# Twenty latency numbers of an order planner, in a hybrid retention and gated-delta layer

## The chip, the cores and the metric

The kernel runs on one core of a Trainium2 chip. The metric is the device time of one execution in microseconds (us), as a median over runs. The core has a matrix engine (TensorE, PE in the profile; its weight loads are PEld), a vector engine (VectorE, DVE), a scalar engine (ScalarE, ACT), a general engine (GpSimd, POOL) and a queue engine (SyncE, SP) that here issues DMAs alone. Each engine works through its own instructions in program order; semaphores hold an instruction until what it needs is there.

## The reference

One decoder layer over 2048 new tokens and, beside them, 8 sample sequences of 8 tokens with states of their own. Half of the heads are retention heads, half gated delta-rule heads; one input projection feeds both, one output projection joins them, and a squared-ReLU MLP follows. Norms stand before and after each half of the layer.

```
h = rmsnorm(x);  q_r, k_r, v_r, gate_r, qkv_g, z_g, a_g, b_g = split(h @ w_in)
retention (4 heads, 128 x 128 state):   q, k rotated by position;  S_t = gamma S_{t-1} + k_t^T v_t;  o_t = q_t S_t
gated delta (4 heads, 128 x 128 state): conv of width 4 and silu on q, k, v;  q, k l2-normed
    g = -exp(A_log) softplus(a + dt_bias);  beta = sigmoid(b)
    S_t = exp(g_t) (I - beta_t k_t k_t^T) S_{t-1} + beta_t k_t v_t^T;  o_t = q_t^T S_t
x = x + rmsnorm([rmsnorm(o_r) silu(gate_r), rmsnorm(o_g) silu(z_g)] @ w_out)
x = x + rmsnorm(square(relu(rmsnorm(x) @ w_up)) @ w_down)
```

Both head groups are computed in chunks. For a chunk of the delta rule the inverse of a triangular matrix I + A is wanted.

## The kernel before

**Tiling.** The 2048 tokens go through in four blocks of 512 (block 0 to 3), each as four chunks or tiles of 128. Block 1 also carries the 64 sample rows, as a fifth tile. A float32 product is made from a rounded part and a remainder (`fhi`, `flo`; `bhi`, `blo`; `ahi`, `alo`; weights as `wpc`), so that three products stand for one; the remainders are made on DVE. All matmuls are issued at L271, all transposes at L275, and most DVE work by helpers at L256 and L259, so tiles rather than lines tell rows apart.

**Two kinds of PE work.** The main stream is the dense work: input projection of a block (`proj`, four kinds of units for four heads), the MLP of the block before it (`mlp`: 8 groups, each an up half and a down half, `mlp_down`, of two units), `out_proj`, and the last MLP group. `merge` interleaves the projection units of block b with the MLP units of block b-1, by which of them may start. Block 0 has no MLP before it, block 3's MLP runs alone at the end. Main products go to three PSUM buffers (`mm`). Beside it run the side steps, small chains that go back and forth between PE and DVE, ACT or POOL: `gdn_head`, `ret_head`, `gdn_sample`, `ret_sample`, `norm2`, `gate_scalars` and others. Their PSUM buffers are the five `mx`, which ACT also uses as scratch when it squares something for a norm.

**What sets the order.** The program is written by a planner, the class `Weave`, that has a clock of its own, `W.t`. The clock runs forward by a fixed cost at each PE product (L271 and L275), and only by these. A side step that has issued its PE products and the other engines' work behind them yields a number, its estimate of the time until its next PE products have their data. When the planner's clock has passed that estimate, the side's next PE products are written into PE's order, between two main products. PE's order is kept as it is written; a product put too early holds the whole of PE back until its data is there, and one put late delays its own chain. DVE's, ACT's and POOL's orders are set by a scheduler, which sees the same program. The estimates stand in the table `TUNE` (L103 to L121), in us of the planner's clock: `first` for block 0, `samp` for block 1, `rest` for blocks 2 and 3.

**The names that the change touches**, each the estimate for the next PE products:

- `inv`: the first transposes of the inverse of a delta-rule head (L834). In blocks 1 to 3, `small_blocks` (L892) makes the inverses of the 16 x 16 diagonal blocks ahead of them, on DVE and by DMAs that POOL issues; its last operations are the products `ym<-ym,cst` and `XX<-XX,ym` on DVE.
- `g5`: the transposes of each further level of that inverse wait a step ahead of the products at L843. In block 0 there are six levels.
- `c1`, `c2`, `c3`: the three steps of the recurrence over chunks, at L866, L871 and L859 (tiles `R`, `vn`, `Sg`).
- `r0`: the first transposes of a retention head (L1148), of the rotated keys (`mt` in blocks 1 to 3, parts of `a`, `flo` and other pages in block 0). DVE rotates them.
- `s3`, `s4`: two steps of the inverse of the sample rows in block 1 (tiles `mss` and `Ys`).
- `h2`: the transposes of a tile after the norm ahead of the MLP (`norm2`, L1349); the tile's pages are `ym`, `XX`, `mt`, `kv` or `a`.

Other gates bear on the prediction. `gate_scalars` makes the decays of all heads of a block (`gp`, `g`) on DVE, after the first `g` unit of `proj`; `ret_sample` needs the rotated sample rows (`qks`). In `out_proj` (L1270) the first three tiles are multiplied with six of the eight heads; the products with the last two heads wait for their outputs, which come through DRAM as `bhi` and `blo`.

The two lines of the planner that decide, in `_step`:

```
w = next(e[1])
e[0] = self.t + w if isinstance(w, float) else w
```

Of the kernel before, what the change touches and what calls it, by code (L numbers as in the profile page):

```python
# [92 lines left out]
def rope_table(nb):  # L93
# [8 lines left out]

TUNE = dict(  # L103
    first=dict(
        conv=7.29, inv=5.0, mem=7.63, pace=0.08, gate=10.83, h2=10.56, rstd=16.8, hk=1.57, put=1.7, gate2=1.82, sc=2.02, gs=9.72,
        g1=2.55, g2=2.75, g3=0.91, g4=2.06, g5=0.58, c1=1.61, c2=1.07, c3=0.99, glate=4.36, s1=7.06, s2=1.58, s3=0.83,
        s4=1.43, s5=0.98, s6=0.86, s7=1.7, r0=2.61, rs=1.89, r1=1.4, r2=2.98, r3=0.73, rlate=6.88, t1=7.35, t2=0.71,
        st=3.5, dg=1.65, n0=0.08, n1=2.49, n2=3.62, n3=1.1, f0=0.1, f1=1.8, f2=1.2),
    samp=dict(
        conv=16.33, inv=44.0, mem=5.28, pace=2.29, gate=12.82, h2=16.26, rstd=0.08, hk=3.65, put=2.29, gate2=1.7, sc=0.68, gs=23.38,  # L110
        g1=2.52, g2=2.04, g3=1.15, g4=1.79, g5=2.54, c1=0.79, c2=1.26, c3=1.4, glate=4.36, s1=4.54, s2=1.63, s3=1.09,
        s4=1.96, s5=1.36, s6=1.13, s7=2.24, r0=1.05, rs=2.27, r1=1.05, r2=1.7, r3=1.68, rlate=4.44, t1=6.0, t2=1.67,
        st=4.16, dg=0.41, n0=0.1, n1=3.78, n2=1.5, n3=1.35, f0=0.1, f1=2.43, f2=1.0),
    rest=dict(
        conv=26.24, inv=40.0, mem=5.1, pace=1.94, gate=16.02, h2=10.82, rstd=20.79, hk=3.86, put=1.19, gate2=1.8, sc=0.53, gs=17.96,
        g1=1.52, g2=1.9, g3=1.26, g4=1.3, g5=1.47, c1=1.22, c2=1.02, c3=0.75, glate=5.39, s1=8.4, s2=3.68, s3=1.36,
        s4=0.84, s5=0.59, s6=1.99, s7=1.22, r0=1.35, rs=1.96, r1=1.15, r2=1.06, r3=1.01, rlate=6.52, t1=9.72, t2=1.51,
        st=6.48, dg=3.52, n0=0.09, n1=2.8, n2=0.84, n3=1.08, f0=0.1, f1=1.15, f2=1.0),
    seq0='g0 r0 v0 q0 q1 v1 q2 g1 v2 r1 q3 v3 g2 r2 g3 r3',
    seq1='q0 q1 g0 r0 v0 g1 r1 v1 g2 q2 r2 v2 q3 g3 r3 v3',  # L120
# [1443 lines left out]
```

## Time and profile before

| | us |
|---|---|
| median of 3 runs | 3024.33 |
| lowest and highest run | 3021.01, 3025.94 |
| the profiled execution | 3030.91 |
| its span in the trace | 3029.1 |
| PE busy | 2879.0 (95%) |
| DVE, ACT, POOL busy | 1443.0, 966.2, 826.9 |
| granted clock of PE, mean | 0.98 |

A span is the time from the first to the last instruction in the trace. In the chain of work that ended last PE holds 77% of the span, DVE 11%, DMA 5%. "Idle" of PE is time between the modelled end of one product and the start of the next; the trace names the engine, tile and line whose result ended it. The granted clock of PE is at one of two levels, 1.0 (2.4 GHz) or 0.50 (1.2 GHz); a stretch that holds both has a value between. Block 0 runs from 0 to about 415 us, with its output projection to 475; block 1 with block 0's MLP to 1172, its output projection to 1285; blocks 2 and 3 to 2660; block 3's MLP to the end.

### The profile page before, as it was taken

The page shows a single profiled execution, that of the slowest core. Times are in us where ns is not written, and L with a number is a line of the kernel's source. Part 1 is how long each engine was busy: PE and PEld are TensorE (multiplying, and loading weights), DVE is VectorE, ACT ScalarE, POOL GpSimd, SP SyncE. Part 2 cuts the span into 40 slices and gives each one's busy share as a digit, 9 for nine tenths or more (in the row PEclk, how much of TensorE's full clock was granted, in tenths as well). Part 3 has the DMA queues.
Part 4 walks back from the last instruction along what each step waited for, and adds up shares of the span by engine and source line. Part 5 has one row for each costly group of instructions (what it writes and reads, how often), then busy time and mean ns, then how long its engine had stood idle before and what let it go on. Part 6 is the DMA issues. An engine that isn't in the chain of part 4 may idle for free.

```text
span 3029.1 us, 43658 instructions
## 1 busy us (share of the span) xinstructions
PE 2879.0 (95%) x16392; PEld 2490.3 (82%) x16392; DVE 1443.0 (48%) x3074; ACT 966.2 (32%) x2573; POOL 826.9 (27%) x970
## 2 busy tenths in 40 slices
PE   7989889899989989899999999999999999999998
PEld 6778788686978779688988989978888888888887
DVE  6655466647483642655254544265353635332113
ACT  4555433233232432332222332332222222221111
POOL 6444232536162541602020211131121212120000
PEclk9999899999999999899999999999999999999999
DMA  8445374656555665764444454675555555665554
GB/s 318 174 160 178 129 273 150 200 187 231 173 196 200 211 222 202 274 224 152 161 161 168 152 193 154 211 257 172 173 193 181 180 180 190 225 246 182 186 195 170
DMA packets 190771, 589.48 MB, mean 195 GB/s; under 512 B 26816, under 2 KB 33344, under 8 KB 190560
## 3 DMA queue, kind: packets, MB, share of 16 engines
q1 hardware_dynamic: 157520, 498.36, 47.6%
q0 software_dynamic: 31888, 86.24, 8.6%
q8 instruction: 129, 2.11, 0.3%
q10 hardware_dynamic: 1152, 2.10, 0.2%
q14 instruction: 82, 0.67, 0.1%
HBM read 443.35 MB, written 138.05 MB: 192 GB/s over the span
## 4 chain that ended last, share of the span: by engine, by line
PE 77%; DVE 11%; DMA 5%; issue 3%; POOL 2%; ACT 2%; SPq 0%; DVEq 0%; POOLq 0%; ACTq 0%
PE mm L271 66%; PE mx L271 8%; PE mx L275 2%; DVE XX L259 1%; DVE ym L259 1%; POOL wpc L259 1%; DVE raw L259 1%; DVE mt L259 1%; DMA x1d<-mt 1%; DMA xin<-in_w_out 1%; DMA wpc<-ws 0%; DVE a L259 0%; DVE flo L259 0%; DMA xin<-in_w_down 0%; DVE blo L256 0%
## 5 line engine op out<-in xcount | busy, mean ns | idle before, releaser
L271 PE MATMUL mm<-ahi,wpc 128*128 128x512 f32 (+2 forms) x3040 | 874.9, 362 | 1.9 <-POOL wpc L259 1.9
L271 PE MATMUL mm<-wpc,fhi 128*128 128x512 f32 x2048 | 659.6, 403 | 17.2 <-POOL wpc L259 7.0
L271 PEld LDWEIGHTS mm<-ahi,wpc 128*128 128x128 f32 x3040 | 542.7, 190 | 81.5 <-issue 6.6
L271 PE MATMUL mm<-alo,wpc 128*128 128x512 f32 (+2 forms) x1520 | 538.1, 354 | 2.0 <-DVE alo L259 2.0
L271 PEld LDWEIGHTS mm<-wpc,fhi 128*128 128x128 f32 x2048 | 382.7, 191 | 106.6 <-POOL wpc L259 9.2
L271 PE MATMUL mm<-bhi,wpc 128*128 128x512 f32 (+2 forms) x1536 | 427.8, 354 | 3.7 <-DMA wpc<-ws 3.7
L271 PE MATMUL mm<-wpc,flo 128*128 128x512 f32 x1024 | 408.6, 399 | 10.3 <-DVE flo L259 10.3
L259 POOL TENSOR_TENSOR wpc<-xin,wpc 128x512 fp32r<-128x512 f32 (+1 forms) x208 | 277.3, 1348 | 190.7 <-ACT wpc L253 180.0
L253 ACT ACTIVATE raw<-mm 128x512 f32<-128x512 f32 (+2 forms) x226 | 114.9, 509 | 633.5 <-PE mm L271 617.4
L271 PEld LDWEIGHTS mm<-alo,wpc 128*128 128x128 f32 x1520 | 288.8, 190 | 34.2 <-DVE alo L259 2.2
L271 PEld LDWEIGHTS mm<-bhi,wpc 128*128 128x128 f32 x1536 | 276.0, 191 | 36.1 <-DMA wpc<-ws 3.9
L271 PE MATMUL mm<-wpc,bhi 128*128 128x256 f32 (+1 forms) x1664 | 295.2, 283 | 1.1 <-ACT bhi L253 1.1
L259 DVE TENSOR_TENSOR a<-a,mm 128x512 f32<-128x512 f32 x224 | 152.5, 685 | 256.1 <-PE mm L271 255.5
L271 PE MATMUL mm<-blo,wpc 128*128 128x512 f32 (+2 forms) x768 | 266.4, 347 | 0.0
L259 DVE TENSOR_TENSOR flo<-raw,fhi 128x512 fp32r<-128x512 f32 (+1 forms) x166 | 108.9, 656 | 330.4 <-ACT raw L253 329.8
L271 PEld LDWEIGHTS mm<-wpc,bhi 128*128 128x128 f32 x1664 | 250.3, 188 | 2.2 <-ACT bhi L253 1.4
L271 PEld LDWEIGHTS mm<-wpc,flo 128*128 128x128 f32 x1024 | 195.2, 191 | 57.3 <-DVE flo L259 12.3
L271 PE MATMUL mm<-wpc,blo 128*128 128x256 f32 (+1 forms) x768 | 214.7, 280 | 0.2 <-DVE blo L259 0.2
L253 ACT ACTIVATE wpc<-xin 128x512 fp32r<-128x512 f32 (+1 forms) x208 | 129.8, 629 | 203.2 <-PE mm L271 119.6
L271 PEld LDWEIGHTS mm<-blo,wpc 128*128 128x128 f32 x768 | 147.4, 192 | 14.7
L271 PEld LDWEIGHTS mm<-wpc,blo 128*128 128x128 f32 x768 | 144.5, 188 | 0.4 <-DVE blo L259 0.4
L253 ACT ACTIVATE XX<-mx 128x512 f32<-128x512 f32 x62 | 36.9, 595 | 305.0 <-PE mx L275 304.9
(504 smaller groups left out, 3965.2 us busy)
## 6 DMA issues: line engine op xcount, KB each, us to landing
wpc<-ws SPq DMA_DIRECT2D x612, 512.0 KB, 5.0
ws<-wpc SPq DMA_DIRECT2D x204, 512.0 KB, 5.7
xin<-in_w_up SPq DMA_DIRECT2D x64, 256.0 KB, 5.4
xin<-in_w_down SPq DMA_DIRECT2D x64, 256.0 KB, 5.4
xin<-in_x_prompt POOLq DMA_DIRECT2D x56, 256.0 KB, 5.0
xin<-in_w_ret SPq DMA_DIRECT2D x28, 256.0 KB, 4.3
mixd<-raw POOLq DMA_DIRECT2D x25, 256.0 KB, 4.4
xin<-mixd POOLq DMA_DIRECT2D x25, 256.0 KB, 4.0
```

Source lines behind the costliest of these rows:

```text
L253: return A.activation(out, in_, f, **kw)
L259: return (eng or V).tensor_tensor(out=out, in0=a, in1=b, op=op)
L271: return tc.keep_in_program_order(nc.tensor.matmul(out, lhsT, rhs, start=start, stop=stop))
L275: return tc.keep_in_program_order(nc.tensor.transpose(out, in_, ident[:rows, :rows]))
```

## The change

Twenty numbers of the table `TUNE` are raised; nothing else is edited. The program has the same products, the same operations on the other engines and the same DMAs. What differs is the place of PE products in PE's order, and by it the order in which the scheduler puts the other engines' work.

```diff
     first=dict(
-        conv=7.29, inv=5.0, ... h2=10.56, ...
-        ... g5=0.58, c1=1.61, c2=1.07, c3=0.99, ...
-        ... r0=2.61, ...
+        conv=7.29, inv=9.5, ... h2=15.0, ...
+        ... g5=1.0, c1=2.0, c2=1.4, c3=1.6, ...
+        ... r0=4.5, ...
     samp=dict(
-        conv=16.33, inv=44.0, ...
-        ... s3=1.09,
-        s4=1.96, ... r0=1.05, ...
+        conv=16.33, inv=50.0, ...
+        ... s3=3.5,
+        s4=4.5, ... r0=4.0, ...
     rest=dict(
-        ... h2=10.82, ...
-        ... r0=1.35, ...
+        ... h2=13.5, ...
+        ... r0=2.6, ...
```

(The first number of a list and its neighbours are shown where they help to find the place; unchanged entries are left out.)

How the order moves is seen in three places. On PE, at the end of block 1's MLP in block 2, `norm2` puts the transposes of its first tile (the page `XX`). Before, they stand right behind a tile of `mlp_down` and ahead of the products of the sample rows (`fs`):

```order
L271 MATMUL mm_18814<-wpc_18743,fhi_17880 128x512 x2
L271 MATMUL mm_18814<-wpc_18743,flo_17881 128x512
L275 MATMUL mx_18844<-cst,XX_18273 128x128 x4
L275 MATMUL mx_18851<-cst,XX_18273 128x128 x4
L271 MATMUL mm_18860<-wpc_18737,fs_17882 128x512 x2
L271 MATMUL mm_18860<-wpc_18739,fs_17882 128x512 x2
L271 MATMUL mm_18860<-wpc_18741,fs_17882 128x512 x2
L271 MATMUL mm_18860<-wpc_18743,fs_17882 128x512 x2
```

and now:

```order
L271 MATMUL mm_18811<-wpc_18740,fhi_17877 128x512 x2
L271 MATMUL mm_18811<-wpc_18740,flo_17878 128x512
L271 MATMUL mm_18841<-wpc_18734,fs_17879 128x512 x2
L271 MATMUL mm_18841<-wpc_18736,fs_17879 128x512 x2
L271 MATMUL mm_18841<-wpc_18738,fs_17879 128x512 x2
L271 MATMUL mm_18841<-wpc_18740,fs_17879 128x512 x2
L271 MATMUL mm_18862<-wpc_18854,fhi_17877 128x512 x2
L271 MATMUL mm_18862<-wpc_18854,flo_17878 128x512
L271 MATMUL mm_18862<-wpc_18856,fhi_17877 128x512 x2
L271 MATMUL mm_18862<-wpc_18856,flo_17878 128x512
L275 MATMUL mx_18871<-cst,XX_18270 128x128 x4
L275 MATMUL mx_18878<-cst,XX_18270 128x128 x4
```

The transposes now have the eight `fs` products and six of the next unit ahead of them.

On PE, in block 1 at its first retention head, the transposes of the rotated keys (`mt`), the first products of the gate (`g`, 128x16) and the transpose of the rotated sample rows (`qks`) stand close together. Before:

```order
L271 MATMUL mm_4837<-bhi_3561,wpc_4831 128x256
L275 MATMUL mx_4850<-cst,mt_4652 128x128 x4
L271 MATMUL mx_4856<-g_4690,cst 128x16
L271 MATMUL mx_4856<-g_4690,Lr 128x16
L271 MATMUL mx_4856<-g_4690,ones 128x16
L275 MATMUL mx_4872<-cst,qks_4653 64x128
```

and now, with ten projection products left out between the two pieces:

```order
L271 MATMUL mx_4853<-g_4690,cst 128x16
L271 MATMUL mx_4853<-g_4690,Lr 128x16
L271 MATMUL mx_4853<-g_4690,ones 128x16
L271 MATMUL mm_4837<-bhi_3561,wpc_4833 128x256
L271 MATMUL mm_4837<-blo_3562,wpc_4833 128x256
L271 MATMUL mm_4837<-bhi_3561,wpc_4833 128x256
L275 MATMUL mx_4872<-cst,qks_4653 64x128
```

```order
L271 MATMUL mm_4882<-bhi_3561,wpc_4829 128x320
L271 MATMUL mx_4889<-g_4690,cst 64x4
L271 MATMUL mx_4889<-g_4690,Lsr 64x4
L271 MATMUL mx_4889<-gb_4859,ones 128x32
L271 MATMUL mx_4897<-Ss_4864,Lsr 64x256 x2
L275 MATMUL mx_4903<-cst,mt_4652 128x128 x4
```

The transposes of `mt` have moved behind the gate's and the sample rows' first steps, which now come first.

On DVE, in block 1 at the end of `small_blocks` of the last head, the last reductions, the accumulations of the MLP's down products (`a<-a,mm`) and the two last operations ahead of the inverse stand so before:

```order
L259 TENSOR_TENSOR a_1108_5499<-a_1108_5499,mm_10489 128x512
L928 TENSOR_REDUCE ym_10049<-ym_10049 128x32
L259 TENSOR_TENSOR ym_10049<-ym_10049 128x512
L996 COPY Ys_10355<-mx_10517 64x64
L928 TENSOR_REDUCE ym_10049<-ym_10049 128x32
L259 TENSOR_TENSOR a_1109_5500<-a_1109_5500,mm_10509 128x512
L259 TENSOR_TENSOR ym_10049<-ym_10049,cst 128x512
L259 TENSOR_TENSOR XX_10007<-XX_10007,ym_10049 128x512
```

and now:

```order
L928 TENSOR_REDUCE ym_10322<-ym_10322 128x32
L259 TENSOR_TENSOR flo_10510<-raw_10677,fhi_10509 128x512
L259 TENSOR_TENSOR XTs_10609<-cst,mx_10696 64x64
L996 COPY Ys_10610<-mx_10709 64x64
L259 TENSOR_TENSOR mss_10611<-mts_10491,cst 64x64
L259 TENSOR_TENSOR flo_10510<-raw_10715,fhi_10509 128x512
L259 TENSOR_TENSOR ym_10322<-ym_10322,cst 128x512
L259 TENSOR_TENSOR Xs_10608<-Xs_10608,mx_10775 64x64
L259 TENSOR_TENSOR XX_10286<-XX_10286,ym_10322 128x512
```

Remainders of an up half and steps of the sample rows stand there in place of the accumulations, which have moved behind `XX`.

## Rows read from the trace of the kernel before

**Rows 1.** Stretches: width, then busy time of PE, PEld, DVE, ACT, POOL, granted clock.

```profile
475.00:1172.00 697.00, 645.64 (x3591) 543.07 (x3591) 386.34 (x811) 242.21 (x633) 308.74 (x329) 0.96 0.59 202
...
1285.00:2660.00 1375.00, 1356.29 (x7839) 1189.18 (x7838) 640.84 (x1398) 403.15 (x1126) 251.02 (x360) 1.00 0.55 185
```

**Rows 2.** Waits of PE, 475 to 1172 us: total, times, longest.

```profile
PE mx L275 <- DVE mt L259: 11.4, 4, 6.1
PE mx L275 <- DVE XX L259: 10.8, 3, 5.6
PE mm L271 <- DVE flo L259: 10.3, 4, 4.7
PE mx L275 <- DVE Ys L996: 5.5, 2, 3.6
PE mx L275 <- issue: 4.0, 1, 4.0
PE mx L275 <- DVE mss L259: 2.3, 1, 2.3
```

**Rows 3.** Waits of PE, 1285 us to the end.

```profile
PE mx L275 <- DVE mt L259: 7.3, 8, 0.9
PE mx L275 <- ACT mx L253: 7.1, 4, 2.4
...
PE mm L271 <- ACT bhi L253: 1.1, 1, 1.1
```

**Rows 4.** Waits of PE, 0 to 475 us.

```profile
PE mx L275 <- DVE XX L259: 5.0, 2, 4.1
PE mx L275 <- DVE ym L256: 4.2, 1, 4.2
PE mx L271 <- DVE Sg L256: 3.9, 3, 2.1
...
PE mx L275 <- DVE flo L259: 2.6, 2, 1.9
PE mx L271 <- ACT XX L253: 2.3, 5, 1.2
```

**Rows 5.** Ten stretches at half clock, their sum; columns as in rows 1.

```profile
sum 47.81, PE 42.05 PEld 34.52 DVE 19.14 ACT 17.76 POOL 18.31; mean PE 4.20 PEld 3.45 DVE 1.91 ACT 1.78 POOL 1.83
```

**Rows 6.** Timeline of PE, block 2: start, duration, instruction, idle before and releaser.

```profile
1502.97 0.66 PE L275 MATMUL mx<-cst,mt 128*128 128x128 f32 x4 [0.91 <-DVE mt L259]
...
1504.87 1.05 PE L271 MATMUL mx<-mt 128*128 128x128 f32 x8
```

**Rows 7.** Timeline of PE, block 2, second norm.

```profile
1973.28 0.66 PE L275 MATMUL mx<-cst,XX 128*128 128x128 f32 x4 [2.43 <-ACT mx L253]
1975.08 1.11 PE L275 MATMUL mx<-cst,XX 128*128 128x128 f32 x4 [1.14 <-ACT mx L253]
```

**Rows 8.** Timeline of ACT beside it.

```profile
1974.31 0.60 ACT L253 ACTIVATE mx<-ym 128x512 f32<-128x512 f32 x1 [1.08 <-DVE ym L256]
```

**Rows 9.** Timeline of DVE, block 1, last head.

```profile
1058.77 6.86 DVE L259 TENSOR_TENSOR flo<-raw,fhi 128x512 fp32r<-128x512 f32 x1 [1.83 <-ACT raw L253]
...
1078.99 0.69 DVE L259 TENSOR_TENSOR a<-a,mm 128x512 f32<-128x512 f32 x1
1084.43 0.69 DVE L259 TENSOR_TENSOR ym<-ym,cst 128x512 f32<-128x512 f32 x1 [4.75 <-DMA ym<-ym]
```

**Rows 10.** Timeline of PE, block 1, first retention head.

```profile
485.85 0.69 PE L275 MATMUL mx<-cst,mt 128*128 128x128 f32 x2 [6.15 <-DVE mt L259]
```

**Rows 11.** Timeline of DVE beside it.

```profile
477.76 1.27 DVE L259 TENSOR_TENSOR gp<-gp,ge 128x20 f32<-128x20 f32 x1
...
481.73 0.18 DVE L259 TENSOR_TENSOR g<-gp,negA 128x20 f32<-128x20 f32 x1
...
485.72 0.21 DVE L259 TENSOR_TENSOR qks<-qks,raw 128x64 f32<-128x64 f32 x1
```

**Rows 12.** Timeline of POOL beside it.

```profile
476.17 5.26 POOL L259 TENSOR_TENSOR wpc<-xin,wpc 128x512 fp32r<-128x512 f32 x4 [7.66 <-ACT wpc L253]
```

More of the change, by code (lines that the diff above doesn't have):

```diff
@@ L104 @@
     first=dict(
-        conv=7.29, inv=5.0, mem=7.63, pace=0.08, gate=10.83, h2=10.56, rstd=16.8, hk=1.57, put=1.7, gate2=1.82, sc=2.02, gs=9.72,
-        g1=2.55, g2=2.75, g3=0.91, g4=2.06, g5=0.58, c1=1.61, c2=1.07, c3=0.99, glate=4.36, s1=7.06, s2=1.58, s3=0.83,
-        s4=1.43, s5=0.98, s6=0.86, s7=1.7, r0=2.61, rs=1.89, r1=1.4, r2=2.98, r3=0.73, rlate=6.88, t1=7.35, t2=0.71,
+        conv=7.29, inv=9.5, mem=7.63, pace=0.08, gate=10.83, h2=15.0, rstd=16.8, hk=1.57, put=1.7, gate2=1.82, sc=2.02, gs=9.72,
@@ L108 @@
+        g1=2.55, g2=2.75, g3=0.91, g4=2.06, g5=1.0, c1=2.0, c2=1.4, c3=1.6, glate=4.36, s1=7.06, s2=1.58, s3=0.83,
+        s4=1.43, s5=0.98, s6=0.86, s7=1.7, r0=4.5, rs=1.89, r1=1.4, r2=2.98, r3=0.73, rlate=6.88, t1=7.35, t2=0.71,
         st=3.5, dg=1.65, n0=0.08, n1=2.49, n2=3.62, n3=1.1, f0=0.1, f1=1.8, f2=1.2),
     samp=dict(
-        conv=16.33, inv=44.0, mem=5.28, pace=2.29, gate=12.82, h2=16.26, rstd=0.08, hk=3.65, put=2.29, gate2=1.7, sc=0.68, gs=23.38,
-        g1=2.52, g2=2.04, g3=1.15, g4=1.79, g5=2.54, c1=0.79, c2=1.26, c3=1.4, glate=4.36, s1=4.54, s2=1.63, s3=1.09,
@@ L112 @@
-        s4=1.96, s5=1.36, s6=1.13, s7=2.24, r0=1.05, rs=2.27, r1=1.05, r2=1.7, r3=1.68, rlate=4.44, t1=6.0, t2=1.67,
+        conv=16.33, inv=50.0, mem=5.28, pace=2.29, gate=12.82, h2=16.26, rstd=0.08, hk=3.65, put=2.29, gate2=1.7, sc=0.68, gs=23.38,
+        g1=2.52, g2=2.04, g3=1.15, g4=1.79, g5=2.54, c1=0.79, c2=1.26, c3=1.4, glate=4.36, s1=4.54, s2=1.63, s3=3.5,
+        s4=4.5, s5=1.36, s6=1.13, s7=2.24, r0=4.0, rs=2.27, r1=1.05, r2=1.7, r3=1.68, rlate=4.44, t1=6.0, t2=1.67,
         st=4.16, dg=0.41, n0=0.1, n1=3.78, n2=1.5, n3=1.35, f0=0.1, f1=2.43, f2=1.0),
@@ L114 @@
     rest=dict(
-        conv=26.24, inv=40.0, mem=5.1, pace=1.94, gate=16.02, h2=10.82, rstd=20.79, hk=3.86, put=1.19, gate2=1.8, sc=0.53, gs=17.96,
+        conv=26.24, inv=40.0, mem=5.1, pace=1.94, gate=16.02, h2=13.5, rstd=20.79, hk=3.86, put=1.19, gate2=1.8, sc=0.53, gs=17.96,
         g1=1.52, g2=1.9, g3=1.26, g4=1.3, g5=1.47, c1=1.22, c2=1.02, c3=0.75, glate=5.39, s1=8.4, s2=3.68, s3=1.36,
-        s4=0.84, s5=0.59, s6=1.99, s7=1.22, r0=1.35, rs=1.96, r1=1.15, r2=1.06, r3=1.01, rlate=6.52, t1=9.72, t2=1.51,
+        s4=0.84, s5=0.59, s6=1.99, s7=1.22, r0=2.6, rs=1.96, r1=1.15, r2=1.06, r3=1.01, rlate=6.52, t1=9.72, t2=1.51,
```

## The prediction

> **What bounds the kernel now.** Read first how PE's time is spread over the stages [rows 1]. In blocks 2 and 3 (1285 to 2660 us) it is busy for 1356.29 of 1375 us at a granted clock of 1.00: little over 18 us are idle, and only the products themselves would be left. In block 1 (475 to 1172) it is busy for 645.64 of 697 us: 51 us are idle, and the clock is 0.96. The dense products are the bound, and what a change of their order alone can win is the idle time between them, and the time in which PE runs at half clock. So the second view is what PE waited for. In block 1 [rows 2] the long entries are transposes (L275) of side steps: the rotated keys (mt), the inverse of a delta head (XX, and one entry "issue"), the sample rows' inverse (Ys, mss). In the rest [rows 3] the list is short: eight times mt, and four waits of the second norm for ACT. In block 0 [rows 4] they are many and small. The third view is the clock [rows 5]: ten stretches of PE at 0.50 that follow waits of the corrected steps. PE was busy for 42.05 us in them; at full clock that work would take half, so up to 21.0 us hang on these waits.
>
> A wait at a side product is a loss since PE goes in written order: main products whose data is there stand behind it. If the estimate is raised, more of these are written ahead of it. The total of products is the same, so the wait is won as far as main products can be put there and as far as nothing else becomes late.
>
> **The change part by part.** I go by the profiled execution, 3030.9 us.
>
> *r0, blocks 2 and 3.* Eight waits of up to 0.9 us, 7.3 together [rows 3]. The order now has six main products more ahead of these transposes. The next step of the same head stands 1.9 us behind the start of the transposes today, with six main products between [rows 6], while the transposes take up to 0.66; so the six take about 1.3 us, over 0.9. Gain 7.3 (bounds 5 to 7.3: a head's later steps move by as much, and the deepest of them gate the next unit).
>
> *h2, blocks 2 and 3.* Four waits, 7.1 us, all at the first tile. The releaser is ACT mx: not the tile XX, but the PSUM buffers that the transposes are written to, which still serve as scratch for squares of the last tile [rows 7, 8]. Of 2.43 + 1.14 us at this place, moving fourteen main products ahead (fourteen times the 0.22 us of such a product, from the six in 1.3) covers 3.1 us, but the buffers now in turn are later ones: the first is that of the square of ym at 1974.31, done some 0.8 us later at 1975.1, against PE's arrival at 1970.85 + 3.1 = 1973.9. Some 1.1 us stay there, and the next square is done about 0.6 us behind it, while the first four transposes take as long: 1.1 to 1.3 us of 3.57 remain in block 2, and some 1.5 in block 3, where twelve products are moved. Gain 4.5 of 7.1 (2 to 7).
>
> *inv, block 1.* Waits on XX, 10.8, and the one named "issue", 4.0: 14.8 us [rows 2]. Why they arise is seen at the last head [rows 9]: the accumulation a<-a,mm at 1078.99 stands between the last DVE operations of the small blocks, and behind it DVE waits 4.75 us for the small blocks' own DMA. The chain ends when its DVE operations, DMAs and the accumulations in front of them are done. In the new order no accumulation stands between the last reduce and the XX operation there, and the estimate is 6 us of planner time longer, over the longest wait of 5.6. What hides it is MLP work of block 0. Gain 13 (5 to 14.8: remainders flo stand between instead).
>
> *s3 and s4, block 1.* Ys 5.5 and mss 2.3, 7.8 us [rows 2]; the raised numbers (2.4 and 2.5 us more) cover most of each but the longest of 3.6. Gain 6 (3 to 7.8).
>
> *r0, block 1.* The waits on mt are 11.4 us, the longest 6.15 at 485.85 [rows 2, 10]. Here the order shows a new first in line: the gate's products (g) and the sample rows' transpose (qks) now stand ahead. DVE makes g at 481.73 and qks at 485.72, done at 485.93 [rows 11], no earlier than mt. PE stood idle from 479.70 on, and only the products between the gate and qks, some 1.4 us, are gained. So 4.7 us of the 6.15 stay under another name. Of the other three (5.3 together) the sample step put ahead leaves about 1.7. Gain 11.4 - 4.7 - 1.7 = 5.0 (1.5 to 11.4).
>
> *Block 0.* XX 5.0 (inv), Sg 3.9 (c3), flo 2.6 (r0), XX from ACT 2.3 (g5): 13.8 us [rows 4]. The longest on Sg, 2.1, and on flo, 1.9, lie at the end of the projections, where no main product is left to be put ahead; 13.8 - 4.0 = 9.8 is gained (0 to 13.8). The second norm's ym, 4.2, has the products of out_proj's last unit and the MLP's first beside it: 4.0 (0 to 4.2).
>
> *The half clock.* Of the 21.0 us at most [rows 5] those go whose wait goes. I take 12: of the 66.4 us of waits above 49.6 are won, which of 21.0 gives 15.7, and new waits will bring some stretches back (bounds 4 to 21.0).
>
> *What is added.* Every estimate that is raised makes its chain longer. In block 1 each delta head's work moves back, and with it the last outputs: the transposes of the last head now stand past the point where out_proj wants its last two heads. Nothing in the trace shows that wait in block 1. The nearest row is the same wait in block 3, bhi, 1.1 us [rows 3]; the far bound is 8, the length of the few DMAs and splits if nothing lies beside them. I take 1.1 (0 to 8). In block 0 the six levels and twelve recurrence steps of the last head run longer into the end of the projections, uncovered: one more of the waits on Sg, 2.1 [rows 4] (-5 to 6). In block 1 the units of the MLP stand in another place against DVE's bursts, and with them the handover from an up half to its mlp_down (flo, 10.3 in four waits [rows 2]); I take one more of mean size, 2.6 (-10.3 to 10.3).
>
> At this place a row speaks against the change. While POOL ran four of its splits from 476.17 on [rows 12], an operation of 128x20 on DVE took 1.27 us, and one of the same form when POOL was done took 0.18 [rows 11]; a remainder flo took 6.86 us at 1058.77 [rows 9]. So a wait that is measured in one order is not a constant of the step: it depends on what DVE and POOL do just then, and a correction by the idle time of one trace can miss in the next. The Trainium skill, page "GPSIMD Engine Reference", section "1. Specifications", says that GpSimd's SBUF interfaces are shared with VectorE and that it contends with VectorE's two-input operations; by it, the re-laid block 1 would draw new waits at other steps, and the sum would end at the slower rival below. The trace agrees that it happens, not that it happens more often.
>
> **Sum.** Gains 7.3 + 4.5 + 13 + 6 + 5.0 + 9.8 + 4.0 + 12 = 61.6; costs 1.1 + 2.1 + 2.6 = 5.8; net 55.8. 3030.9 - 55.8 = 2975.1. The profiled execution is 6.6 us over the median of 3024.3, so the forecast is 2968.5, told as 2969.
>
> **Rivals.**
>
> *Waits handed on.* In blocks 0 and 1 each wait that is removed shows up at the next product that needs DVE, as with g and qks above; then only blocks 2 and 3 win: 7.3 + 4.5 and two half-clock stretches behind the second norm at 2.1 each (21.0 over ten [rows 5]), 4.2: 16.0, so 3008. For it: PE's waits in block 1 are mostly for DVE, whose work is the same. Against: DVE is busy for 386.34 of 697 us there [rows 1], so it is late at places, not throughout.
>
> *Slower.* The re-laid block 1 sets each of the 14 units of mlp_down behind a burst of DVE work, in which the remainders flo are slow beside POOL. Each then waits like the longest now, 4.7 [rows 2], and loses 2.1 by a half-clock stretch (21.0 over ten): 14 x 6.8 = 95.2, less the 10.3 of today, 84.9; less the gain of 55.8, 29 us more: 3053. It decides from (55.8 + 10.3) / 6.8, that is from 10 units of 14 on. Against: four such waits stand in the trace now, and about as many handovers lie inside bursts in the new order.
>
> *Nothing happens.* The numbers are in the planner's clock; if DVE's own order moved back with PE's, the waits would stay as they are: 3024, within 6 us. Against: DVE's rows at the last inverse have moved ahead of the accumulations, not with them.
>
> *All of it.* Each gain at its upper bound and no new cost: 7.3 + 7 + 14.8 + 7.8 + 11.4 + 13.8 + 4.2 + 21.0 = 87.3, so 2937.
>
> **How the numbers follow.** Forecast (gain 35 to 75, 2949 to 2989) 0.55; more than that, down to 2937, 0.08; handed on (gain 7 to 35, 2989 to 3017) 0.23; nothing 0.05; slower 0.09. From 2937 to 3015 lie the first two and most of the third, some 0.84. A measurement of this kernel tells 0.2%, 6 us, from no change. Faster by more than that: 0.55 + 0.08 + 0.22 = 0.85; within it 0.06; slower 0.09.
>
> **What would show it.** In the new trace the eight waits on mt of blocks 2 and 3 are gone; the second norm's first tile there waits for ACT 1 to 1.5 us; in block 1 the XX and Ys waits are near nothing, while a wait of 4 to 5 us near 486 us names g or qks; out_proj of block 1 shows a wait for bhi of about 1 us; half-clock stretches are fewer. I would be wrong if block 1's idle time stays near 50 us with new names (handed on), or if flo waits appear at most units of mlp_down (slower), or if block 0 ends later than today because its chains have grown.

## The result, and the profile after

| | before | after |
|---|---|---|
| median, us | 3025.14 (4 runs) | 2989.93 (4 runs, 2987.78 to 2994.72) |
| ratio, 95% interval | 1 | 0.9889 [0.9877, 0.9902] |
| span of the profiled execution | 3029.1 | 2992.9 |
| PE busy | 2879.0 | 2869.1 |

The change makes the kernel 35 us faster (1.1%), where a gain of 55.8 was forecast; the interval lies wholly under 1. In the profiled executions the span falls by 36.2 us: PE's busy time by 9.9 (the same products), its idle time by 26.3. The diff raises thirteen numbers, not the twenty that the title and the text on the change speak of: seven of block 0, four of block 1, two of blocks 2 and 3.

The stages by the same program points (start of a block's projection, of its output projection, of its own MLP; block 0's output projection lies ahead of the first). Stretches of before, block 1 and then all from block 1's MLP on; columns as in rows 1, with the share of the DMA engines and GB/s behind the clock:

```profile
410.00:1172.10 762.10, 702.48 (x4005) 599.18 (x4004) 427.83 (x941) 262.06 (x687) 316.14 (x340) 0.96 0.59 203
...
1267.30:3029.00 1761.70, 1733.09 (x9559) 1499.66 (x9557) 738.13 (x1556) 480.25 (x1270) 277.33 (x395) 1.00 0.56 189
```

and of after, the same two:

```profile
400.20:1149.00 748.80, 697.67 (x3998) 594.52 (x3998) 435.90 (x935) 260.59 (x681) 313.02 (x336) 0.96 0.58 203
...
1242.30:2992.80 1750.50, 1729.49 (x9559) 1497.29 (x9557) 741.68 (x1560) 478.62 (x1272) 280.53 (x396) 1.00 0.56 190
```

Block 0 (up to the first of these) is 9.8 us shorter, block 1 13.3, its output projection 1.9 and the rest 11.2. A trace is of one run: block 0 with the numbers of before took 409.9 to 414.8 us in four traces, so a stage's length is known to some 5 us. PE still idles for 51.1 us in block 1 (748.80 - 697.67), after 59.6, and its clock there is the same 0.96. The larger part of what block 1 won lies at its start. From the point on that was at 475 us in before [rows 1], the stretch in after is

```profile
457.40:1149.00 691.60, 643.58 (x3585) 540.91 (x3585) 394.91 (x805) 240.79 (x627) 304.55 (x325) 0.96 0.58 202
```

with 48.0 us idle, after 51.4. What PE waits for there has new names. Waits of PE in after, 450 to 1160 us (total, times, longest), against [rows 2]:

```profile
PE mx L275 <- DVE kv L256: 21.7, 4, 5.8
PE mx L275 <- DVE Ys L996: 12.2, 2, 6.7
PE mx L275 <- DVE qks L259: 5.0, 3, 2.7
PE mm L271 <- DVE flo L259: 2.4, 2, 1.3
...
PE mx L271 <- DVE g L259: 2.2, 1, 2.2
```

XX, mt and "issue" are gone, 26.2 us, and mss, 2.3. In their place stands kv, which was in none of the rows of before: the last transposes of a retention head (L1179), four heads, 5.2 to 5.8 us each. Ys has doubled. In blocks 2 and 3, against [rows 3]:

```profile
PE mx L275 <- ACT mx L253: 3.6, 2, 1.8
PE mx L275 <- DVE kv L256: 2.6, 2, 2.1
```

The eight waits on mt are gone, the second norm's are halved.

**Where a kv wait comes from.** The first of the four, on PE (start, duration, instruction, idle before and releaser):

```profile
501.11 1.26 PE L275 MATMUL mx<-cst,kv 128*128 128x128 f32 x4 [5.20 <-DVE kv L256]
```

DVE beside it:

```profile
491.53 0.37 DVE L256 SCALAR_TENSOR_TENSOR sor<-sor,cst 128x4 f32<-128x4 f32 x1
...
493.63 1.96 DVE L256 SCALAR_TENSOR_TENSOR ogs<-ogs,sos,vds 64x128 f32<-64x128 f32 x1
...
495.59 1.35 DVE L263 TENSOR_SCALAR vzs<-raws,cw 128x64 f32<-128x64 f32 x1
496.98 1.22 DVE L256 SCALAR_TENSOR_TENSOR vzs<-raws,cw,vzs 128x64 f32<-128x64 f32 x1
...
500.71 1.13 DVE L256 SCALAR_TENSOR_TENSOR kv<-kv,sor,ym 128x128 f32<-128x128 f32 x4
```

and POOL:

```profile
493.65 1.03 POOL L259 TENSOR_TENSOR fs<-vds,cst 64x512 f32<-64x512 f32 x1
494.65 1.06 POOL L259 TENSOR_TENSOR sor<-sor,mhalf 128x4 f32<-128x4 f32 x1
495.64 2.47 POOL L259 TENSOR_TENSOR wpc<-xin,wpc 128x512 fp32r<-128x512 f32 x2
```

The head's norm goes DVE (sor), POOL (its power of -1/2), DVE (four products kv). POOL reached the power at 494.65, behind splits and masks; and between sor and kv DVE had 13 other operations in its order, those of the sample rows and of the next unit's conv, some of them slow. In the three other heads 8 operations stand between, of usual length; slow ones stand ahead of sor. With r0 at 1.05, in the experiment below, it is 1 or 2. In before, kv came 1.5 us behind sor at this head (506.07 and 507.60).

**Where a Ys wait comes from.** On DVE, then on POOL, then on PE, near 900 us:

```profile
894.21 6.88 DVE L259 TENSOR_TENSOR ym<-ym 128x256 f32<-128x256 f32 x1
901.01 0.20 DVE L996 COPY Ys<-mx 64x64 f32<-64x64 f32 x1
```

```profile
894.54 6.16 POOL L259 TENSOR_TENSOR wpc<-xin,wpc 128x512 fp32r<-128x512 f32 x5
```

```profile
901.26 0.31 PE L275 MATMUL mx<-cst,Ys 64*64 64x64 f32 x1 [5.58 <-DVE Ys L996]
```

A DVE operation of the small blocks took 6.88 us while POOL ran five remainders of MLP weights one behind the other; it ended 0.4 us after them, and the copy of Ys stood behind it. The longest wait on Ys in before, 3.6 us at 728.67, had such an operation ahead of its copy too:

```profile
720.10 7.94 DVE L259 TENSOR_TENSOR ym<-ym 128x256 f32<-128x256 f32 x1 [0.17 <-DMA ym<-xf]
...
728.41 0.21 DVE L996 COPY Ys<-mx 64x64 f32<-64x64 f32 x1
```

**The clock.** After these waits PE runs at half clock (second wait on kv; sum over the seven stretches that follow kv, Ys and the gate):

```profile
668.40:678.64 10.24, 6.67 (x15) 4.24 (x16) 4.21 (x11) 1.63 (x3) 1.97 (x4) 0.50 0.33 131
...
sum 61.45, PE 45.36 PEld 34.30 DVE 36.07 ACT 13.90 POOL 13.29; mean PE 6.48 PEld 4.90 DVE 5.15 ACT 1.99 POOL 1.90
```

Half of 45.36, 22.7 us, is what they cost beside the waits themselves. Over the whole span, the sum of all stretches at half clock in before (22) and in after (18):

```profile
sum 122.99, PE 98.03 PEld 82.45 DVE 55.21 ACT 35.51 POOL 42.54; mean PE 4.46 PEld 3.75 DVE 2.51 ACT 1.61 POOL 1.93
sum 119.52, PE 92.10 PEld 73.92 DVE 64.84 ACT 37.33 POOL 43.84; mean PE 5.12 PEld 4.11 DVE 3.60 ACT 2.07 POOL 2.44
```

The half clock costs nearly the same: half of PE's busy time in it is 49.02 us before and 46.05 after.

### The profile page after: what moved, and what is told of

It is laid out like the page before. It is cut to its first block, busy times and chain, and to the rows that moved or that the text cites. A ratio compares the mean times of both kernels' runs of the same rounds, so it can differ in the third digit from the quotient of the medians.

```text
span 2992.9 us, 43660 instructions
## 1 busy us (share of the span) xinstructions
PE 2869.1 (96%) x16392; PEld 2488.7 (83%) x16392; DVE 1457.3 (49%) x3074; ACT 963.9 (32%) x2573; POOL 825.9 (28%) x968
## 4 chain that ended last, share of the span: by engine, by line
PE 79%; DVE 9%; DMA 4%; issue 3%; POOL 2%; ACT 2%; SPq 0%; DVEq 0%; POOLq 0%; ACTq 0%
PE mm L271 68%; PE mx L271 9%; PE mx L275 2%; DVE XX L259 1%; DVE ym L259 1%; POOL wpc L259 1%; DMA x1d<-mt 1%; DMA xin<-in_w_down 1%; DVE a L259 0%; DMA xin<-in_x_prompt 0%; DMA xin<-in_xpT 0%; DMA XX<-ym 0%; DVE vz L256 0%; ACT junk L253 0%; DVE vzs L256 0%
## 5 line engine op out<-in xcount | busy, mean ns | idle before, releaser
L259 POOL TENSOR_TENSOR a<-a,vz 128x512 f32<-128x512 f32 x28 | 36.5, 1318 | 339.3 <-ACT mx L253 339.0
```

Source lines behind the costliest of these rows:

```text
L259: return (eng or V).tensor_tensor(out=out, in0=a, in1=b, op=op)
```

## The experiments

Eleven kernels, by median; the kernel before had 3026.34 in the first four's comparison, 3025.98 in the next four's, 3023.33 in the last three's. Differences between kernels of different comparisons are known to no better than these 3 us.

| kernel | us | ratio to before, 95% interval |
|---|---|---|
| blocks 2 and 3's numbers alone | 3016.23 | 0.9969 [0.9957, 0.9982] |
| block 0's alone | 3009.85 | 0.9948 [0.9927, 0.9968] |
| block 1's alone | 3016.46 | 0.9969 [0.9957, 0.9980] |
| the change without block 1's r0 | 2972.07 | 0.9821 [0.9803, 0.9840] |
| ... and without s3, s4 | 2983.85 | 0.9874 [0.9851, 0.9896] |
| the change, rlate up | 2998.40 | 0.9922 [0.9901, 0.9943] |
| without r0, s4, s7 and rlate up | 3010.01 | 0.9954 [0.9939, 0.9968] |
| without r0, MLP remainders on DVE | 2938.68 | 0.9725 [0.9708, 0.9741] |
| before, MLP remainders on DVE | 2978.63 | 0.9856 [0.9840, 0.9871] |
| the change, MLP remainders on DVE | 2941.72 | 0.9730 [0.9716, 0.9745] |
| without r0, all remainders on DVE | 2948.09 | 0.9749 [0.9729, 0.9769] |

**Each block's numbers alone.** Edits to the kernel before:

```diff
+    rest: h2=13.5, r0=2.6                                           (blocks 2, 3)
```

> The kernel before with the two numbers of blocks 2 and 3 alone raised (h2 10.82 to 13.5, r0 1.35 to 2.6). In the traces of before and after the same products of blocks 2 and 3 (from the end of out_proj of block 1 on) lie 23.7 us apart at their start and 36.2 at the end, so 12.5 us were won in these blocks. Theory of parts (each group of numbers wins in its own block alone): 12 to 14 us faster than before. Rival (parts help or hurt each other through the shifted order): off from that by 5 us or more.

```diff
+    first: inv=9.5, h2=15.0, g5=1.0, c1=2.0, c2=1.4, c3=1.6, r0=4.5   (block 0)
```

> The kernel before with the seven numbers of block 0 alone raised. In the two traces block 0's last norm transposes lie 14.3 us apart (441.60 and 427.30). Theory of parts: 13 to 15 us faster than before. Rival: the earlier end of block 0 is given back in block 1, whose DVE work then falls otherwise: under 8 us.

```diff
+    samp: inv=50.0, s3=3.5, s4=4.5, r0=4.0                            (block 1)
```

> The kernel before with the four numbers of block 1 alone raised (inv, s3, s4, r0). Block 1 and its output projection won 9.4 us between the traces of before and after; of these 3.7 are a wait for a weight DMA at its start that is gone. Theory of parts: 5 to 10 us faster than before, with four waits on kv of 5.2 to 5.8 us (21.7 in sum) and two on Ys (12.2) as in the trace of after, in place of those on mt (11.4) and XX (10.8, and 4.0 issue). Rival: without the changes of block 0 the bursts of DVE fall elsewhere and these waits aren't there: over 20 us faster.

Measured: 10.1, 16.5 and 9.9 us faster, 36.5 together, against 35.2 of the whole change. The parts add up within their intervals (some 5 us each way), and block 0's gain isn't given back in block 1. Blocks 2 and 3 came a little under what was expected, though in every profile with just these numbers there the stretch from block 1's MLP to the last product is 11 to 14 us shorter than in before, and 0 to 3 without them. With block 1's numbers alone the four new waits on kv are there too (455 to 1172 us), so they are not made by block 0's earlier end; of the two on Ys that were expected one came, and another tile of the sample rows, Xs, stands in place of the other:

```profile
PE mx L275 <- DVE kv L256: 21.9, 4, 5.8
PE mx L275 <- DVE Ys L996: 5.6, 1, 5.6
PE mx L271 <- DVE Xs L259: 5.0, 1, 5.0
```

**Block 1's r0 taken back.** Edit to the changed kernel:

```diff
-    samp: r0=4.0
+    samp: r0=1.05
```

> The changed kernel with block 1's r0 back at 1.05. Theory (handed on through DVE's order): the later r0 moves the last four DVE operations of a retention head (kv<-kv,sor,ym) behind the sample rows' and the conv's operations, so it makes the four kv waits, 21.7 us; without it they go and the waits on mt come back, 11.4 in before: 8 to 12 us faster than the changed kernel, some 45 faster than before. Rival (the four kv waits come from the other numbers of block 1): they stay, and the mt waits come on top: about 10 us slower than the changed kernel, 25 faster than before.

18 us faster than the changed kernel, 54 faster than before: more than the theory's 8 to 12, and on the other side of the rival's. Waits of PE, 450 to 1140 us, and the stretch of block 1:

```profile
PE mx L275 <- DVE mt L259: 11.4, 4, 6.1
PE mx L271 <- POOL fs L259: 6.4, 5, 2.0
PE mx L275 <- DVE Ys L996: 5.8, 2, 4.1
```

```profile
398.70:1127.80 729.10, 691.25 (x4000) 591.05 (x3999) 443.77 (x936) 261.96 (x681) 317.51 (x338) 0.98 0.60 209
```

kv is gone, mt is back as in before. Idle time in block 1 is 37.9 us (after: 51.1), and PE's busy time falls by 6.4 to 691.25, at a clock of 0.98 for 0.96: the waits of over 5 us took a part of the clock with them. So of the change's four numbers in block 1 this one cost 18 us, and the other three, by subtraction, won some 28.

**s3 and s4 taken back as well.**

```diff
-    samp: s3=3.5, s4=4.5, r0=4.0
+    samp: s3=1.09, s4=1.96, r0=1.05
```

> The changed kernel with block 1's r0, s3 and s4 back at 1.05, 1.09 and 1.96, so that of block 1 only inv is changed. Theory (the Ys waits come from DVE operations that are held for 5 to 9 us while POOL makes splits, and not from the estimate): the waits on Ys and mss stay between 4 and 12 us, and the time is within 6 us of the 2972 with s3 and s4 raised. Rival (the estimates were short by the idle time read): Ys and mss come back with 7.8 us or more and the time is 8 to 12 us over 2972. In either case inv alone keeps the waits on XX under 2 us.

Neither: the time is the rival's, 12 us over 2972, and the waits are not. PE waits 1.3 us on Ys here and on mss not at all, less than with the raised estimates; another of the sample rows' tiles, Xs, makes PE wait 3.3 (455 to 1160 us):

```profile
PE mx L271 <- DVE Xs L259: 3.3, 1, 3.3
...
PE mx L271 <- DVE Ys L996: 0.9, 1, 0.9
...
PE mx L275 <- DVE Ys L996: 0.4, 1, 0.4
```

The stretch of block 1:

```profile
396.80:1141.60 744.80, 704.01 (x4004) 600.73 (x4003) 433.17 (x941) 263.39 (x687) 321.78 (x340) 0.95 0.59 206
```

PE idles for 40.8 us, 2.9 more than with s3 and s4 raised, and is busy for 12.8 more, at 0.95 of full clock. The half clock is the difference: 68.3 us of this stretch are at half clock, with PE busy for 59.8 of them, where the kernel with s3 and s4 raised has 34.1 and 33.3, and less half of that both are busy for 674 us. But this varies from run to run of one kernel. The four runs here go from 2976.54 us, at a mean clock of 0.986, to 2990.33 at 0.980, and the trace is of the last; the four with s3 and s4 raised lie between 2969.81 and 2972.67 at 0.986 or 0.987. So at a like clock the two are some 4 to 7 us apart, by their medians 12; s3 and s4 are worth something between 4 and 20 us, and why the clock varies isn't shown. For inv, the one number of block 1 that is raised here: XX waits 2.4 us, a little over the 2 that were expected, of 14.8 with "issue" in before.

**More of the same correction.** kv and the rest corrected by the idle time that the new trace shows:

```diff
-    samp: rlate=4.44
+    samp: rlate=10.5
```

> The changed kernel with block 1's rlate raised from 4.44 to 10.5, its r0 left at 4.0. If the four kv waits (21.7 us) are there since the last DVE operations of a retention head now stand behind 5 to 7 us of other DVE work, six planner us more in front of their transposes cover them: kv waits near nothing, 18 to 24 us faster than the changed kernel, 2966 to 2972. Rival (each delay hands the wait on to the next chain): new waits at mlp_down's flo, at Ys or at out_proj take 10 us or more of it.

The theory missed: 8 us slower than the changed kernel, though kv no longer waits. Block 1 itself does become shorter, 706.3 us for 748.8. But the retention heads' later ends push the rest of the chains past the last projection product, and the stretch of out_proj, 93.3 us in after, is

```profile
1101.70:1242.30 140.60, 114.23 (x665) 97.27 (x664) 61.36 (x118) 38.92 (x119) 45.73 (x59) 0.81 0.43 155
```

with 26 us idle and 0.81 of full clock: the last chain has no main products to cover it. The two stretches together are 4.8 us longer, with 4.9 less idle and 9.7 more busy, so that more of it lies in the clock than in the waits. (The traces, of runs of 2992.43 us here and 2994.72 in after, show where time moved, and not the 8 us between the medians.) The rival had the size right, with out_proj the one place of its three that counts.

```diff
-    samp: r0=4.0, s4=4.5, s7=2.24        rest: rlate=6.52
+    samp: r0=1.05, s4=8.0, s7=4.3        rest: rlate=8.8
```

> The changed kernel with block 1's r0 back at 1.05, its s4 at 8.0 and s7 at 4.3, and rlate of blocks 2 and 3 at 8.8 (from 6.52). Theory of covering: the waits on Ys (5.8) and fs (6.4) in block 1 and on kv in blocks 2 and 3 (2.6) shrink to a third: 6 to 12 us under 2972. Rival (which DVE operation is held changes with every order): the sum of PE's idle time in block 1 stays within 5 us, with other names, and the time within 5 us of 2972.

38 us slower than without these raises, outside both. Block 1 is 10.5 us longer (739.6 for 729.1), and from its MLP to the last product it is 31 (1773.7 for 1742.7). Waits of PE from 2480 us on, in block 3:

```profile
PE mx L275 <- ACT XX L253: 2.8, 1, 2.8
...
PE mx L271 <- DVE R L256: 1.9, 4, 0.6
PE mx L271 <- ACT vn L253: 1.6, 4, 0.4
PE mx L271 <- DVE Sg L256: 1.3, 3, 0.4
```

The last delta head's whole recurrence (R, vn, Sg for each chunk) now runs with nothing beside it, from 2552 us to 2574, and PE is at half clock from 2559 to 2583; all for a correction of waits on kv of 2.6 us, which are still there (2.8 us).

**POOL's remainders moved to DVE.** In the kernel before, DVE makes the remainders of the activations; those of the weights (`wpc`) are made on POOL, as [rows 12] show, and not on DVE as the text on the tiling has it. Edit to the kernel without block 1's r0, in load_unit:

```diff
-                tt(lo, r, hi.bitcast(F32), ALU.subtract, eng=G)
+                tt(lo, r, hi.bitcast(F32), ALU.subtract, eng=V if name in ("w_up", "w_down") else G)
```

> The changed kernel with block 1's r0 back, and with the remainders of the MLP's weights (wpc, first load) made on DVE in place of POOL. Theory (POOL's two-input operations hold DVE): the some 24 DVE operations over 1.4 us in block 1, 85 us in sum, go nearly all; DVE does 128 more operations of about 0.68 us. The waits on Ys, fs and flo shrink; the time is between 15 us faster and 10 us slower than 2972, depending on how late DVE's chains become by 87 us more work. Rival (the long DVE operations have another cause, such as a semaphore or DMA traffic): as many operations over 1.4 us as now.

33 us faster than 2972, better than the best that was expected, and the fastest kernel of the study, level with the changed kernel under the same edit below. DVE's operations over 1.4 us in block 1, counted in its timeline: 24 with 77.2 us in sum in before, 22 with 80.0 in after, 24 with 85.4 without r0, and 3 with 4.8 here. Groups of DVE in block 1 (busy, mean ns), in after:

```profile
L259 DVE TENSOR_TENSOR flo<-raw,fhi 128x512 fp32r<-128x512 f32 x29 | 29.8, 1029 | 28.6 <-ACT raw L253 28.5
L259 DVE TENSOR_TENSOR ym<-ym 128x256 f32<-128x256 f32 x16 | 28.7, 1795 | 5.6 <-DMA ym<-xf 5.3
```

and here, with the block's stretch below:

```profile
L259 DVE TENSOR_TENSOR wpc<-xin,wpc 128x512 fp32r<-128x512 f32 x120 | 84.4, 710 | 24.4 <-ACT wpc L253 23.4
...
L259 DVE TENSOR_TENSOR flo<-raw,fhi 128x512 fp32r<-128x512 f32 x29 | 20.4, 705 | 19.4 <-ACT raw L253 19.2
...
L259 DVE TENSOR_TENSOR ym<-ym 128x256 f32<-128x256 f32 x16 | 9.9, 618 | 4.3 <-DMA ym<-xf 4.1
```

```profile
396.90:1095.80 698.90, 681.21 (x4001) 585.85 (x3999) 415.78 (x1056) 261.73 (x681) 159.69 (x218) 0.99 0.62 219
```

DVE took on 84.4 us of work, and its busy time in block 1 fell by 28 (443.77 to 415.78). The same operation on ym took 618 ns in place of 1795. PE's order is that of the kernel without r0, product for product. So the long operations of DVE are made by POOL's remainders. Not all of the 33 us need come from them: POOL's busy time in block 1 falls from 317.51 to 159.69 us, and PE's waits on POOL's own results (fs, wpc) from 8.2 to 0.9. No run parts the two.

**The same edit on the kernel before and on the changed kernel.**

> The kernel before, with all its numbers, and the remainders of the MLP's weights made on DVE in place of POOL. If the holds of DVE by POOL and the early estimates are separate causes, the edit is worth what it was with the new numbers, 33 us (2972 to 2939): 2992, and the waits on XX and mt of block 1 stay at 10 us or more each. If the waits that the change corrects were themselves made by held DVE operations, the waits on XX, Ys, mss and flo in block 1 (33 us together with the one named issue) go to under 12 without any change of a number, and the time is under 2982.

45 us faster than before: by its time the second case, by its waits half of each. Those on Ys, mss and flo are gone (455 to 1130 us), so POOL's remainders made them, and 4.1 of the 11.4 on mt; those on XX and "issue" stay, 13.9 us:

```profile
PE mx L275 <- DVE XX L259: 9.8, 2, 9.0
PE mx L275 <- DVE mt L259: 7.3, 4, 2.5
PE mx L275 <- issue: 4.1, 1, 4.1
```

The estimate of inv was short in itself; that of Ys wasn't. The longer wait on XX, on PE, and what stands in front of it on DVE:

```profile
1034.98 1.12 PE L275 MATMUL mx<-cst,XX 128*128 128x128 f32 x4 [9.00 <-DVE XX L259]
```

```profile
1029.12 0.69 DVE L928 TENSOR_REDUCE ym<-ym 128x32 f32<-128x512 f32 x1
1033.51 0.69 DVE L259 TENSOR_TENSOR ym<-ym,cst 128x512 f32<-128x512 f32 x1 [3.71 <-DMA ym<-ym]
```

> The changed kernel, its r0 of block 1 at 4.0, with the remainders of the MLP's weights on DVE. If the four kv waits come from where DVE's order puts the last operations of a retention head, they stay, 15 to 22 us, and it is some 15 to 20 us slower than the same with r0 at 1.05 (2939): 2955 or so. If they come from DVE operations that POOL holds, they fall under 6 us, and the two are within 6 us of each other.

The second case by its time, 3 us from the kernel with r0 back, and between the two by its waits (455 to 1110 us):

```profile
PE mx L275 <- DVE kv L256: 10.8, 4, 5.8
```

Half of the 21.7 is gone without a change of the order on PE: three of the four waits are down to 1.5 to 1.9 us, and the last head's stays at 5.8. So half came with POOL's remainders, and 10.8 us are left that they don't make, more than the 7.3 on mt that raising r0 saves under this edit. With the remainders on DVE the thirteen numbers are worth 37 us (2978.63 to 2941.72), as much as without.

**All remainders on DVE.**

```diff
-  eng=V if name in ("w_up", "w_down") else G
+  eng=V
```

> As the kernel with r0 back and the MLP's remainders on DVE (2939), and with all other weights' remainders on DVE too (76 operations in block 0). If POOL holds DVE in block 0 as in block 1, block 0's waits of PE for POOL's wpc and for DVE shrink: 5 to 15 us faster, under 2934. Rival: in block 0 the chains between PE and DVE are what bounds it, and 50 us more DVE work there makes it slower: 2940 to 2955.

The rival's range: 9 us slower than 2938.68, though the two intervals overlap; faster by 5 to 15 it is not. Block 0 itself got hardly shorter (block 1's projection starts at 395.8 us for 396.9), and the way from there to the first MLP product took 95.0 us for 88.0. Which of block 0's chains became late isn't settled by this run.

## Why the prediction was right, and where it was not

The time lies in the range and the sign is right, but 2989.93 stands on the border between the case that was forecast (2949 to 2989) and "waits handed on" (2989 to 3017). By its terms, in us:

| term | predicted | measured in the traces |
|---|---|---|
| r0, blocks 2, 3 | 7.3 | mt 7.3 gone, kv 2.6 new: 4.7 |
| h2, blocks 2, 3 | 4.5 | 7.1 to 3.6: 3.5 |
| inv, block 1 | 13 | 14.8, all |
| s3, s4 | 6 | 7.8 to 12.2: -4.4 |
| r0, block 1 | 5.0 | 11.4 to 28.9 (kv, qks, g): -17.5 |
| block 0, with its cost of 2.1 | 11.7 | idle 49.5 to 42.0, ym behind it 4.2 to 2.2: 9.5 |
| half clock | 12 | half of PE's busy time in it, 49.02 to 46.05: 3.0 |
| out_proj's heads, block 1 | -1.1 | blo 0.2 new: -0.2 |
| mlp_down's flo | -2.6 | 10.3 to 2.4: 7.9 |
| sum | 55.8 | 21.3 |

The other 15 us of the 36.2 stand in no term. Of these, 3.7 are a wait for a weight's DMA that is gone (at 415.93 us in before), 2.6 are idle time in block 1's output projection, and some 7 are busy time of PE, most of it in block 0, that the half clock doesn't account for and whose cause stays open. The terms alone would give some 3004 us, in the range still but in the middle of "handed on"; that the time came to the border of the case that was forecast is luck.

- **What bounds the kernel, and where a gain can lie:** right. The order alone won idle time, and each block's numbers won time of their own.
- **Block 1:** the terms of its waits and costs (inv, s3 and s4, r0, out_proj, flo) came to 20.3 us in the forecast and to 0.6 in the trace. The prediction's own sign of being wrong, block 1's idle time near 50 us with new names, came true: 48.0 after 51.4. Here the rival "handed on" had it right; blocks 0, 2 and 3 came near the forecast.
- **Blocks 2 and 3:** right in kind. The second norm waits 1.74 and 1.83 us where 1.1 to 1.5 was foretold, since the buffers, not the tile, are late, as read from [rows 7, 8].
- **inv:** right, the estimate was short: the waits stay when only POOL's remainders are moved and fall to 2.4 us when inv alone is raised in block 1. The reason given holds in part. The DMA of the small blocks makes DVE wait in both kernels (4.75 us [rows 9], 3.71 us); an accumulation among the last operations isn't needed, since in the kernel before with the remainders on DVE none stands behind the last reduction, and PE waits 9.0 us.
- **r0, block 1:** this step failed. It followed the transposes to the next products in line, and there it was close: g and qks wait 7.2 us, where 4.7 and 1.7 were left. It did not follow the head to its end. "Every estimate that is raised makes its chain longer" was priced for block 1's chains at out_proj alone, where 0.2 us came; with r0 raised by 2.95 us of planner time the head's last DVE operations met the next unit's conv and the sample rows in DVE's order. Taking r0 back shows what it cost: 18 us, waits and half clock together.
- **s3, s4:** this step failed too. The wait was priced as an estimate that is 3.6 us short. The longest of the three stood behind a DVE operation held by POOL (at 720.10, above), and all three are gone when POOL's remainders are moved. The prediction had the rows that said so [rows 9, 11, 12], and the sentence that a wait measured in one order is no constant of the step, but gave it to a rival with 0.09 and not to the terms. The Trainium skill, page "SBUF — State Buffer", section "Who interferes with whom", states that a DVE instruction with two SBUF inputs contends with a GpSimd instruction that reads SBUF; the trace agrees (6.88 us for an operation of 0.6).
- **The half clock:** mis-sized. The time at half clock hardly fell, from 123 us to 120, and 3.0 us came back: the new waits of over 5 us, with the seven stretches above, brought nearly as much as went. The ten stretches of [rows 5] are 47.8 of the 123 us. Without r0 it is 75 us in all.
- **The slower rival** did not come: flo waits fell. Its mechanism, DVE operations slow beside POOL's work, was real, and hit kv and Ys in place of mlp_down.

## What to carry to other kernels

A wait that a trace shows at one step is a fact of that order; before an estimate is corrected by it, look at what the releasing engine did just then: if the operation that ended the wait took ten times its usual time, or stood behind work of others, a later place will meet another such moment, and the cause is to be removed instead. Here that was worth 45 us alone, more than the thirteen numbers. And a chain that is delayed is delayed to its end: follow it to its last operation on every engine, and to the place where main work runs out.

## What the runs showed of the hardware

- POOL's two-input operations can hold a DVE operation for as long as POOL has them back to back: 6.88 us over five in a row, 8.44 us for another of the same form, against 0.6. It isn't always so: beside four in a row [rows 12] DVE got four operations of some 1.2 us through, one of them the 1.27 of [rows 11], and beside two in a row DVE ran two of 1.35 and 1.22 us (at 495.59). What decides isn't shown. How many operations over 1.4 us there are hardly depends on the order (22 to 24 in block 1, 77 to 85 us, in three orders); which chain they hit does, and so does what PE loses.
- Moving 84.4 us of such work from POOL to DVE made DVE's total busy time less, by 28 us.
- PE's half clock is a price of its own beside idle time, and it varies from run to run: two traces whose idle time in block 1 differs by 2.9 us differ by 12.8 us in PE's busy time for the same products, and four runs of one kernel go from 2976.54 us at a mean clock of 0.986 to 2990.33 at 0.980.
